# A hybrid attention layer on one Trainium2 core: where the DRAM additions, the branch operands' splits and the output slots stand in the attention steps

## The chip, the cores and the metric

The kernel runs on one core of a Trainium2 chip. The metric is the device time of one execution in microseconds: the median of three runs before the change is 1536.99 us (1536.19 to 1539.3). One further execution was taken with the hardware profiler; it took 1535.65 us.

## The reference

One layer over 1024 frames of width 1024. `h` is the RMS-normed input, and one projection gives all mixers' operands:

```
z = h @ w_in;  qa, fa, ia, ga, qb, kb, vb, gate_a, gate_b = split(z)
oa = hgrn2(qa, fa, ia, ga)                       # gated linear recurrence, 4 heads, chunks of 64
ob = band_attention(qb, kb, vb, ...)             # 8 heads of 64; each chunk sees itself and 8 chunks back
x  = x + (sigmoid(gate_a) * (oa @ w_branch_a) + sigmoid(gate_b) * (ob @ w_branch_b)) @ w_out
x  = x + (silu(h2 @ w_ffn_gate) * (h2 @ w_ffn_up)) @ w_ffn_down
x  = x + sigmoid(h3 @ w_ple_gate) * (p @ w_ple_proj)
```

In band attention q and k are RMS-normed per head, the scores get a relative-position bias, and a softmax over at most 576 keys is multiplied with v. All is in float32.

## The kernel before, in words

**Products in three parts.** Each float32 operand is kept as a rounded high part and a remainder ("hi" and "lo", type float32r), and a product is three matmuls: hi*hi, hi*lo, lo*hi. So each operand has to be split: a cast on ScalarE (ACT) for hi and a subtraction for lo on VectorE (DVE) or GpSimd (POOL).

**The order is written out by hand.** The helpers `order` (line 93), `load`, `mul`, `tr` and the pinned engines `V`, `A`, `G` chain every instruction to the one issued before it on the same engine, so PE, ACT, DVE, POOL and the DMA queue of SyncE (SP) each run in exactly the order in which the Python code emits the instructions. Semaphores between engines are made by the framework. PSUM has eight banks, handed out by `mm`; working tiles of 128x1024 come from 32 "slots", handed out by `slot`.

**The attention stage** (`attention`, line 787) is a loop over steps n = 0 to 33. Steps 0 to 31 each treat one pair of heads and one block of 128 queries: pairs 0 and 1 alternate in steps 0 to 15, pairs 2 and 3 in steps 16 to 31, and the block number grows every second step, so that steps 16 to 31 repeat the shapes of steps 0 to 15. A step emits, in this order: the loads for later steps; the rest of the softmax of step n-1; a **first unit** of the feed; the scores of step n (`scores`); in odd steps the products with v of steps n-3 and n-2 (`pv`); the transposes of q and k of step n+1 (`stack`); the splits due in this step; a **second unit** of the feed; the transposes of the probabilities of step n-1 (`pt`) and the exponentials of step n. I write 20a and 20b for the first and the second unit of step 20.

**The feed** is a stream of matmul work that fills PE between the small attention products. It gives first the q/k projection (`attn_in`, line 691; the rest of it lasts through step 19) and then `branch_a` (line 1172): `oa @ w_branch_a`, 32 units of 6 matmuls, each 128x512. After each unit, `tick` (line 199) advances all pending side jobs in `self.later` by one piece. What the loop leaves of the feed is run by `branches` (line 1199) after it. In steps 20 and 21 (`SINGLE`) the first unit is left out and only `tick` is called.

**Side jobs.** `qk_norm` (line 669) norms one finished 128x512 block k of the q/k projection: squares on ACT; one tick later a reduction on DVE and a power of -0.5 on POOL (shape 128x8); two ticks after that the row scaling on DVE, which reads the PSUM bank for the last time; two ticks later the block is stored. Blocks that finish together (k = 0, 1; 6, 7; 8, 9; 14, 15) start `late` ticks apart. `split_in` (line 895) casts a loaded head output on ACT and appends the DVE subtraction as a side job that waits for `slack`, which is set in the first half of a step. `fetch` (line 169) does the same for weights.

**Operands of branch_a.** The four head outputs `oa` were stored to DRAM; `load_in` loads them again into four slots at the end of step 13, and `SPLITS` says in which steps they are split: 18, 19, 19 and 20. The attention's own outputs `ob` take one slot for each pair of heads, at the scores of its first block (steps 0, 1, 16, 17), though the first write to it comes with `pv`, in steps 3 and 19.

**DRAM additions.** The out-projection and the down-projection need sums of quarters of their weights. `dma_sums` (line 1346) first copies quarters from DRAM to DRAM (issued by SP) and then adds others on top, with DMAs issued from POOL:

```
add = lambda out, x: self.G.dma_start(out, x, accum_op=ALU.add, max_dma_last_dim=4 * T)
```

`next(self.adds)` issues one such addition: at the start of each odd step, and in `branch_a` at the start of each of its four parts (the first of them just ahead of its first unit). Since POOL's order is fixed, a power of `qk_norm` that is emitted behind an addition can't run before that addition is issued.

Of the kernel before, what the change touches and what calls it, by code (L numbers as in the profile page):

```python
# [22 lines left out]
HALF = 512  # L23
NFF = 22
STEPS = (NFF // 2 + 1) // 2
SPLITS = (18, 19, 19, 20)
EPS = 1e-6
LEVELS = (1, 2, 4, 8, 16)
TURN = 32
# [2 lines left out]
LATE = 8  # L32
FIRST = 5
PRE = {1: (0, 1), 2: (2, 3), 9: (4, 5), 10: (6, 7)}
SINGLE = (20, 21)
GROUPS = ((0, 1), (2,), (3,), (4,), (5,), (6, 7))
RING = 4
RAW = 2
# [39 lines left out]
class Trunk:  # L78
# [612 lines left out]
    def attn_in(self):  # L691

        self.qkd = [self.spill() for _ in range(8)]
        for two in range(2):
            ws = []
            for blks in GROUPS:
                pss = []
                for j, _ in enumerate(self.tokens(ws or self.lazy(ws), blks, pss)):
                    if blks[0] == 6 and (j % 2 if two == 0 else j == 3):
                        self.fetch()  # L700
                    yield 1296
                self.later += [self.qk_norm(8 * two + b, ps, i) for i, (b, ps) in enumerate(zip(blks, pss))]

    def qk_load(self, k):
        if k < 16:
# [81 lines left out]
    def attention(self):  # L787

        steps = [(2 * two + p, b) for two in range(2) for b in range(8) for p in range(2)]
        whole = len(steps)  # L790
        feed = chain(self.feed, self.ticked(self.branch_a()))
        sc, pts = {}, {}

        def stack(n):
            if n >= whole:
                return iter(())
            p, b = steps[n]
            if b == 0:
                for h in range(2):
                    bt = self.small(640, tag="bias")  # L800
                    self.load(bt, self.d["bias"][2 * p + h])
                    self.bias[p, h] = bt
            return self.attn_stack(p, b)

        def scores(n):
            for h, stages in enumerate(self.attn_scores(*steps[n])):
                sc[n, h] = (*next(stages), stages)

        def stage(n, h):
            if 0 <= n < whole:  # L810
                next(sc[n, h][2], None)

        def pt(n, h):
            if 0 <= n < whole:
                pts[n, h] = self.attn_pt(*sc[n, h][:2])

        def pv(n):
            if 0 <= n < whole:
                self.attn_pv(*steps[n], (pts.pop((n, 0)), pts.pop((n, 1))), sc[n, 0][1])

        self.stacks = True
        self.qk_load(0)
        for i in range(4):
            next(feed, None)
            if i == 0:
                self.hgrn_gate()
            if i == 3:
                drain(stack(0))
                drain(self.hgrn_out())
        self.adds = chain(self.osum, self.wsum)  # L830
        while self.queue:
            self.rest()
        self.queue = None
        bsrc = []
        for n in range(whole + 2):
            if n % 2 and n < whole:
                next(self.adds)
            if n % 2 == 0:
                self.qk_load(n // 2 + 1)
                next(self.copies, None)  # L840
                next(self.copies, None)
            stage(n - 1, 1)
            self.slack = True
            if n in SINGLE:
                self.tick()
            else:
                next(feed, None)
            if n < whole:
                if steps[n][1] == 0:
                    self.ob.append(self.slot())  # L850
                scores(n)
            if n % 2:
                pv(n - 3)
                pv(n - 2)
            drain(stack(n + 1))
            for _ in range(SPLITS.count(n)):
                self.osrc.append(self.split_in(raws[len(self.osrc)]))
            if n in (whole - 4, whole - 3):
                bsrc.append(self.split_in(braws[len(bsrc)]))
            if n == whole:  # L860
                bsrc += [(self.slot(F32R), self.slot(F32R)) for _ in range(2)]
                self.split_half(bsrc, 0)
            self.slack = False
            next(feed, None)
            pt(n - 1, 1)
            stage(n, 0)
            stage(n, 1)
            pt(n - 1, 0)
            stage(n, 0)
            if n == 0:  # L870
                self.keep_heads(self.oa, self.od, self.done_heads)
            if n == whole // 2 + 1:
                self.keep_heads(self.ob, self.obd, [0, 1])
            if n == whole // 2 - 3:
                raws = self.load_in(self.od)
            if n == whole // 2 + 4:
                for _ in range(2):
                    self.gate_load()
            if n == whole - 6:
                braws = self.load_in(self.obd[:2])  # L880
            yield 0
        self.slack = True
        self.split_half(bsrc, 1)
        for _ in range(2):
            self.gate_load()
        self.bsrc, self.feed = bsrc, feed
# [1353 lines left out]
def drain(stream):  # L2240
    while True:
        try:
            next(stream)
        except StopIteration as e:
            return e.value
# [125 lines left out]
```

## Time and profile before

| | |
|---|---|
| median of 3 runs | 1536.99 us (1536.19 to 1539.3) |
| the profiled execution | 1535.65 us, span of its instructions 1533.7 us |
| PE / DVE / ACT / POOL busy in the span | 1510.9 / 1135.4 / 662.0 / 641.2 us |
| mean granted clock of PE | 0.998 |
| chain that ended last | PE 86%, DVE 7%, issue 3%, ACT 2%, DMA 1%, POOL 1% |

Times in the views are microseconds from the first instruction. PE is the matmul engine, PEld its weight load, SPq the queue of SyncE. In a row of the timeline stand the start, the duration, the engine, the line, the operation, out<-in by the program's tile names (`pm` a PSUM bank, `s` a slot, `m` a small tile, `wh`/`wl` and `whi`/`wlo` the two parts of weights, `d` DRAM), the shapes, a count, and in brackets the idle time before it and the instruction that ended it. In a row of the windows view stand the stretch, its length, the busy time of PE, PEld, DVE, ACT and POOL with counts, the granted clock, the DMA engines' share and GB/s. Most instructions carry line 75 or 107, which are helpers.

### The profile page before, as it was taken

What the parts mean: (1) busy time and instruction counts of PE and PEld (TensorE: products, weight loads), DVE (VectorE), ACT (ScalarE), POOL (GpSimd) and SP (SyncE); (2) the same over time, 40 slices, a digit from 0 to 9 for tenths busy, and PEclk for the clock granted to TensorE, in tenths of its full rate; (3) what the DMA queues carried; (4) which work ended last, traced back from release to release, by engine and by line L of the source; (5) the groups of instructions that cost most, each with busy time, mean ns of one, the idle gap of its engine ahead of it and who ended that gap; (6) DMA issues with size and microseconds to landing.
All of it is one profiled execution on the core that took longest, in us unless ns stands there. A gap on an engine that the chain in (4) does not pass through costs nothing.

```text
span 1533.7 us, 20820 instructions
## 1 busy us (share of the span) xinstructions
PE 1510.9 (99%) x7680; PEld 1246.9 (81%) x7680; DVE 1135.4 (74%) x1616; ACT 662.0 (43%) x1115; POOL 641.2 (42%) x365
## 2 busy tenths in 40 slices
PE   8999999999999998999999999999999999999998
PEld 6888888888887876888888888888888888888886
DVE  5778777666676767848998877777777667756678
ACT  6634333333327666733566322222222224446452
POOL 4237334500122212045223666665555545545546
PEclk9999999999999999999999999999999999999999
DMA  5557445785749779574445344443333288785325
GB/s 209 191 174 266 144 145 185 292 319 172 282 143 261 217 193 250 120 249 136 137 156 197 108 120 127 124 124 104 103 103 103 105 308 297 282 278 197 125 100 202
DMA packets 106548, 281.73 MB, mean 184 GB/s; under 512 B 11088, under 2 KB 15952, under 8 KB 105936
## 3 DMA queue, kind: packets, MB, share of 16 engines
q1 hardware_dynamic: 97600, 256.29, 47.7%
q0 software_dynamic: 8704, 24.12, 7.8%
q8 instruction: 60, 0.98, 0.3%
q14 instruction: 40, 0.33, 0.1%
q10 hardware_dynamic: 144, 0.02, 0.0%
HBM read 205.67 MB, written 106.17 MB: 203 GB/s over the span
## 4 chain that ended last, share of the span: by engine, by line
PE 86%; DVE 7%; issue 3%; ACT 2%; DMA 1%; POOL 1%; SPq 0%; DVEq 0%; ACTq 0%; POOLq 0%
PE pm L107 84%; DVE s L75 4%; PE pm L110 2%; ACT s L75 1%; DVE wl L155 0%; ACT m L75 0%; DMA wr<-in_qk 0%; DVE m L75 0%; DMA s<-in_x 0%; ACT wh L147 0%; POOL wl L155 0%; DVE q L75 0%; POOL m L75 0%; DMA wr<-in_pp 0%; DMA wr<-d 0%
## 5 line engine op out<-in xcount | busy, mean ns | idle before, releaser
L107 PE MATMUL pm<-s,whi 128*128 128x512 f32 x1904 | 586.5, 389 | 0.6 <-DVE t L75 0.6
L107 PE MATMUL pm<-s,wh 128*128 128x512 f32 (+1 forms) x1456 | 453.2, 392 | 7.4 <-ACT wh L147 5.3
L107 PEld LDWEIGHTS pm<-s,whi 128*128 128x128 f32 x1904 | 357.1, 188 | 75.4 <-DVE t L75 1.3
L107 PE MATMUL pm<-s,wlo 128*128 128x512 f32 x952 | 370.6, 389 | 0.2 <-DVE wlo L75 0.2
L75 DVE TENSOR_TENSOR s<-s,s 128x512 f32<-128x512 f32 (+3 forms) x246 | 295.6, 1232 | 64.7 <-ACT s L75 50.3
L107 PEld LDWEIGHTS pm<-s,wh 128*128 128x128 f32 x1456 | 271.8, 189 | 64.9 <-ACT wh L147 5.3
L107 PE MATMUL pm<-s,wl 128*128 128x512 f32 (+1 forms) x728 | 284.0, 390 | 0.5 <-POOL wl L155 0.5
L155 POOL TENSOR_TENSOR wl<-wr,wh 128x1024 fp32r<-128x1024 f32 (+3 forms) x71 | 176.8, 2494 | 218.6 <-ACT wh L147 213.0
L75 DVE TENSOR_TENSOR t<-pm,t 128x512 f32<-128x512 f32 x168 | 115.7, 689 | 128.6 <-PE pm L107 103.7
L107 PEld LDWEIGHTS pm<-s,wlo 128*128 128x128 f32 x952 | 178.7, 188 | 38.0 <-DVE wlo L75 0.9
L75 POOL TENSOR_TENSOR wlo<-wr,whi 128x1024 fp32r<-128x1024 f32 (+1 forms) x67 | 143.4, 2148 | 67.0 <-ACT whi L75 58.0
L107 PEld LDWEIGHTS pm<-s,wl 128*128 128x128 f32 x728 | 137.3, 189 | 29.6 <-POOL wl L155 1.2
L75 POOL TENSOR_TENSOR wlo<-q,whi 128x512 fp32r<-128x512 f32 x66 | 107.8, 1635 | 117.5 <-ACT whi L75 64.4
L147 ACT CAST wh<-wr 128x1024 fp32r<-128x1024 f32 (+2 forms) x82 | 81.1, 991 | 159.8 <-DMA wr<-d 49.2
L75 ACT CAST s<-s 128x1024 fp32r<-128x1024 f32 (+1 forms) x112 | 106.9, 976 | 64.9 <-DMA s<-d 26.6
L75 ACT CAST whi<-q 128x512 fp32r<-128x512 f32 (+1 forms) x99 | 75.0, 758 | 110.8 <-PE pm L107 87.0
L75 POOL TENSOR_TENSOR s<-t,rb 128x512 f32<-128x512 f32 x44 | 71.1, 1618 | 98.7 <-ACT t L75 98.7
L75 POOL TENSOR_TENSOR m<-m,mhalf 128x8 f32<-128x8 f32 (+1 forms) x24 | 35.9, 1520 | 158.4 <-DVE m L75 158.4
L75 ACT ACTIVATE t<-s 128x512 f32<-128x512 f32 x44 | 27.8, 632 | 159.5 <-DVE s L75 155.2
L107 PE MATMUL pm<-whi,s 128*128 128x512 f32 x256 | 91.8, 409 | 0.0
L107 PE MATMUL pm<-wh,s 128*128 128x512 f32 x256 | 88.1, 403 | 0.0
L75 DVE TENSOR_TENSOR s<-s,pm 128x512 f32<-128x512 f32 x72 | 45.5, 683 | 31.5 <-PE pm L107 31.5
(156 smaller groups left out, 1932.4 us busy)
## 6 DMA issues: line engine op xcount, KB each, us to landing
s<-d SPq DMA_DIRECT2D x81, 512.0 KB, 6.3
d<-s SPq DMA_DIRECT2D x46, 512.0 KB, 3.6
d<-s SPq DMA_DIRECT2D x87, 256.0 KB, 2.3
wr<-d SPq DMA_DIRECT2D x36, 512.0 KB, 3.5
d<-t SPq DMA_DIRECT2D x54, 256.0 KB, 4.1
wr<-in_sz SPq DMA_DIRECT2D x24, 512.0 KB, 6.7
wr<-in_sg SPq DMA_DIRECT2D x22, 512.0 KB, 3.8
wr<-in_su SPq DMA_DIRECT2D x22, 512.0 KB, 4.4
```

The source lines that it names most:

```text
L75: return lambda *a, **k: self.trunk.order(op(*a, **k), self.key)
L107: return self.order(self.nc.tensor.matmul(*a, **k))
L110: return self.order(self.nc.tensor.transpose(*a, **k))
L147: self.nc.scalar.copy(hi[:, c], raw[:, c])
L155: rest.tensor_tensor(lo[:, c], raw[:, c], f32(hi[:, c]), ALU.subtract)
```

## The change

Five edits in one place of the program:

- The addition of each odd step is issued at the end of the step and no longer at its start. The four additions of `branch_a` stay where they are in it.
- `SINGLE` goes: steps 20 and 21 have a first unit like all others, so `branch_a` begins with 20a and no longer 20b, and two units fewer are left for `branches`.
- The head outputs are loaded at the end of step 11 (before: 13) and split in steps 14, 16, 18 and 19 (before: 18, 19, 19, 20).
- A slot for `ob` is taken at the first `pv` of a pair of heads and no longer at its first scores.
- In `attn_in`, the second of two blocks that finish together (k = 1, 7, 9, 15) starts its `qk_norm` two ticks after the first and no longer one.

```
-SPLITS = (18, 19, 19, 20)
+SPLITS = (14, 16, 18, 19)
...
-SINGLE = (20, 21)
...
-                self.later += [self.qk_norm(8 * two + b, ps, i) for i, (b, ps) in enumerate(zip(blks, pss))]
+                self.later += [self.qk_norm(8 * two + b, ps, 2 * i) for i, (b, ps) in enumerate(zip(blks, pss))]
...
         def pv(n):
             if 0 <= n < whole:
+                if steps[n][1] == 0:
+                    self.ob.append(self.slot())
                 self.attn_pv(*steps[n], (pts.pop((n, 0)), pts.pop((n, 1))), sc[n, 0][1])
...
         for n in range(whole + 2):
-            if n % 2 and n < whole:
-                next(self.adds)
             if n % 2 == 0:
                 self.qk_load(n // 2 + 1)
                 next(self.copies, None)
                 next(self.copies, None)
             stage(n - 1, 1)
             self.slack = True
-            if n in SINGLE:
-                self.tick()
-            else:
-                next(feed, None)
+            next(feed, None)
             if n < whole:
-                if steps[n][1] == 0:
-                    self.ob.append(self.slot())
                 scores(n)
...
             stage(n, 0)
+            if n % 2 and n < whole:
+                next(self.adds)
...
-            if n == whole // 2 - 3:
+            if n == whole // 2 - 5:
                 raws = self.load_in(self.od)
```

Here `whole` is 32.

## The prediction

> **What bounds the kernel now.** I read the page first, then the windows view and the timelines of the attention stage.
>
> ```profile
> PE 1510.9 (99%) x7680; PEld 1246.9 (81%) x7680; DVE 1135.4 (74%) x1616; ACT 662.0 (43%) x1115; POOL 641.2 (42%) x365
> ```
>
> PE is busy for 99% of the span, so only time in which PE waits, or runs slowly, can be won. The attention loop has a built-in comparison: steps 18 to 26 have the shapes of steps 2 to 10. These windows run from the scores of step 2 to those of step 11, and from the scores of step 18 to those of step 27:
>
> ```profile
> 473.49:522.05 48.56, 47.69 (x349) 37.50 (x348) 36.80 (x125) 35.80 (x97) 10.93 (x9) 1.00 0.86 226
> 566.59:620.67 54.08, 48.57 (x338) 37.00 (x337) 39.59 (x126) 38.07 (x98) 11.87 (x11) 0.97 0.95 270
> ```
>
> The second has less matmul work (338 records against 349, because 20a and 21a are left out) and takes 5.52 us more. What a unit is worth, from the four units ahead of the loop, which lie between these two rows:
>
> ```profile
> 457.93 0.47 PE L107 MATMUL pm<-whi,s 128*128 128x512 f32 x1
> ...
> 463.50 1.26 PE L110 MATMUL pm<-eye,m 128*128 128x128 f32 x10
> ```
>
> 24 matmuls in 463.50 - 457.93 = 5.57 us make 1.39 us for a unit of six. At the first window's pace the second would take 48.56 - 2 x 1.39 = 45.78 us, so it loses 54.08 - 45.78 = **8.30 us**. Where (steps 20 and 21, two parts of step 22, then steps 4 and 5):
>
> ```profile
> 574.07:579.29 5.22, 4.04 (x19) 2.37 (x18) 4.56 (x13) 5.03 (x13) 0.21 (x1) 1.00 1.07 331
> 579.29:585.87 6.58, 6.28 (x43) 4.58 (x44) 6.12 (x21) 6.06 (x18) 0.83 (x1) 1.00 1.06 352
> 589.10:593.40 4.30, 0.55 (x3) 0.34 (x4) 2.17 (x4) 0.48 (x1) 4.30 (x4) 0.96 0.80 119
> 593.40:596.65 3.25, 3.25 (x9) 2.33 (x9) 3.10 (x12) 1.99 (x5) 0.93 (x2) 0.53 0.75 166
> 482.15:487.26 5.11, 4.51 (x25) 3.20 (x25) 4.14 (x13) 5.11 (x16) 0.00 (x0) 1.00 0.90 231
> 487.26:492.81 5.55, 5.55 (x43) 4.29 (x42) 4.78 (x14) 4.04 (x14) 4.45 (x3) 1.00 1.02 316
> ```
>
> In step 22 PE works for 0.55 of 4.30 us, and then for 3.25 us at a granted clock of 0.53. Step 20 loses 5.22 - (5.11 - 0.60 - 1.39) = 2.10 us against step 4 (0.60 is PE's idle time there, 5.11 - 4.51), and step 21 loses 6.58 - 5.55 = 1.03 against step 5, together 3.1; the rest, some 5 us, is step 22. What held it up, on POOL and then on DVE:
>
> ```profile
> 559.52 1.66 POOL L75 TENSOR_TENSOR m<-m,mhalf 128x8 f32<-128x8 f32 x1 [9.61 <-DVE m L75]
> 561.15 1.08 POOL L75 DMA_DIRECT2D d<-in_wq  x1
> 568.55 1.05 POOL L75 DMA_DIRECT2D d<-in_wq  x1 [6.32 <-issue]
> 579.08 1.04 POOL L75 DMA_DIRECT2D d<-in_wq  x1 [9.48 <-issue]
> 588.31 1.05 POOL L75 DMA_DIRECT2D d<-in_wq  x1 [8.19 <-issue]
> 588.89 3.78 POOL L75 TENSOR_TENSOR m<-m,mhalf 128x8 f32<-128x8 f32 x2
> 583.19 0.23 DVE L75 TENSOR_SCALAR m<-m,m 128x8 f32<-128x8 f32 x1
> 591.09 0.69 DVE L75 TENSOR_TENSOR m<-pm,m 128x512 f32<-128x512 f32 x1 [3.89 <-POOL m L75]
> ```
>
> The four DMA rows are the additions of steps 17, 19, 20b and 21. The first three were this long on the way:
>
> ```profile
> DMA to landing us min/median/max: 7.1/7.1/7.1
> DMA to landing us min/median/max: 10.2/10.2/10.2
> DMA to landing us min/median/max: 8.9/8.9/8.9
> ```
>
> 561.15 + 7.1, 568.55 + 10.2 and 579.08 + 8.9 each lie some 0.3 us ahead of the next issue: an addition of this kind isn't issued until the one before it has landed, and POOL stands still meanwhile. The powers of blocks 14 and 15 (x2, 588.89) stand behind the addition of step 21. Block 14's input was ready at 583.4; DVE stood 3.89 us for its power, with the softmax behind it.
>
> **The change part by part.**
>
> *Additions at the end of the step.* The same DMAs on the same queue, moved past the powers of their own step alone. By ticks, block 14 is now squared in 20a, has its power in 20b and is scaled in 21b; block 15 (two ticks behind) has its power in 21b. POOL's order becomes: addition of 19, addition of 20a, power 14, power 15, addition of 21. The addition of 20a still waits for the one of 19, until 579.08, and frees POOL at 580.1. When is power 14 due? Block 6 has the same ticks in steps 4 and 5:
>
> ```profile
> 487.01 0.23 DVE L75 TENSOR_SCALAR m<-m,m 128x8 f32<-128x8 f32 x1
> 491.78 0.68 DVE L75 TENSOR_TENSOR m<-pm,m 128x512 f32<-128x512 f32 x1
> ```
>
> Its input is ready 5.1 us and its scaling due 9.6 us behind the scores of step 4 (482.15). With 20a in front, the scores of step 20 come at 574.07 + 1.39 = 575.5, so block 14's input is ready at 580.6, its power (1.66) done at 582.2 and due at 585.1: hidden with some 2.9 us to spare, and POOL is free by 580.1 in time. Power 15 has no addition ahead of it that isn't ahead of power 14. Late next are the addition of 21 and those behind it, for which only additions wait. So the stall of step 22 goes, with its slow clock; without the cover up to all of its 5 us stays.
>
> *Splits earlier.* Each is a cast on ACT and a subtraction on DVE:
>
> ```profile
> 572.85 1.99 ACT L75 CAST s<-s 128x1024 fp32r<-128x1024 f32 x2
> 576.60 2.35 DVE L75 TENSOR_TENSOR s<-s,s 128x1024 fp32r<-128x1024 f32 x2
> ```
>
> So 1.0 and 1.2 us. The subtractions run in the first half of the next step: before in 19, 20 (two) and 21, after in 15, 17, 19 and 20. Two of them, 2.4 us of DVE, leave steps 20 and 21. Where they go there is room:
>
> ```profile
> 552.59 0.35 DVE L75 SCALAR_TENSOR_TENSOR s<-pm,cols,s 128x128 fp32r<-128x128 f32 x1 [1.40 <-ACT m L75]
> 564.36 0.35 DVE L75 SCALAR_TENSOR_TENSOR s<-pm,cols,s 128x128 fp32r<-128x128 f32 x1 [2.85 <-ACT m L75]
> 545.99 0.48 ACT L75 COPY m<-pm 128x384 f32<-128x384 f32 x1 [1.09 <-PE pm L110]
> 558.38 0.48 ACT L75 COPY m<-pm 128x384 f32<-128x384 f32 x1 [0.52 <-PE pm L110]
> ```
>
> In steps 15 and 17 DVE idles 1.40 and 2.85 us right behind the place. The casts meet 1.09 us of idle ACT in step 14 and 0.52 in step 16, where half a microsecond is pushed on. Cost: nothing; without the cover 1.2 us each.
>
> *First units in 20 and 21* bring 2.78 us of PE work forward from `branches`: nothing in sum. The one of 20a also fills the hole ahead of the scores of step 20. Of the 3.1 us of steps 20 and 21 all could stay (one subtraction remains in 20) or none. DVE's load decides; steps 4 to 7 and 20 to 23:
>
> ```profile
> 482.15:503.91 21.76, 21.16 (x157) 16.46 (x156) 16.13 (x55) 16.60 (x49) 5.55 (x4) 1.00 1.00 259
> 574.07:603.04 28.97, 23.46 (x151) 16.99 (x150) 21.40 (x67) 18.85 (x51) 7.90 (x7) 0.94 0.89 229
> ```
>
> Steps 20 to 23 will need 21.40 - 2.4 = 19.0 us of DVE, and their twins take 21.76 us. That fits at 87%, with little to spare, so I leave a third, **1.0 us** (bounds 0 and 3.1).
>
> *Slots and loads.* The four loads of `oa` move by two steps on SP,
>
> ```profile
> 528.20 1.87 SPq L102 DMA_DIRECT2D s<-d  x4
> ```
>
> 1.87 us of issue past one load of q and k and two copies, none of them due in the same step. By my count of the code, the projection's input 16, v 4, k 4, `ob` 2, loaded outputs 4 and two hi parts make just 32 slots in step 16; `ob` of pair 2, taken at its scores, would be the 33rd. Taken at `pv`, it isn't. Cost: nothing; at worst half a step, some 2.5 us, if my count is one short.
>
> *Blocks 1, 7, 9 and 15 a tick later.* Each holds its PSUM bank half a step longer. Blocks 0 and 1 pass in the recurrence, ahead of the loop:
>
> ```profile
> 431.65 0.67 DVE L75 TENSOR_REDUCE m<-m 128x8 f32<-128x512 f32 x1
> 433.35 1.29 DVE L75 TENSOR_TENSOR s<-s,s 128x512 f32<-128x512 f32 x2
> 434.80 1.16 PE L107 MATMUL pm<-s,m 128*128 128x128 f32 x8 [1.30 <-ACT m L75]
> ```
>
> Their two reductions take 433.35 - 431.65 = 1.70 us of DVE, and PE waits 1.30 us behind them. One now goes behind the next level: up to 0.85 us won, or up to a unit, 1.39 us, lost if the bank is missed. I take half of the 0.85, **0.4 won**. For blocks 7 and 9 the first window holds 48.56 - 47.69 = 0.87 us of PE idle in all; I leave it (bounds: all won, or as much again lost).
>
> **The sum.** 8.30 - 1.0 + 0.4 = 7.7 us. Behind the loop PE has no gaps to speak of,
>
> ```profile
> 660.31:1533.70 873.39, 865.32 (x3852) 715.69 (x3850) 652.36 (x674) 339.86 (x455) 447.47 (x236) 1.00 0.49 166
> ```
>
> so the gain should reach the end. The profiled execution took 1535.65 us (1533.7 of span, 1.95 around it) and would take 1527.9; the median of the runs lies 1.34 above it: 1536.99 - 7.7 = **1529.3 us**. With all bounds at once the gain is between 8.30 - 3.1 - 2.5 - 1.39 - 0.87 = 0.4 and 8.30 + 0.85 + 0.87 = 10.0; not all of them hold together, and leaving the slot's 2.5 aside, my own range for this case is 2.9 to 10.0.
>
> A rule of the Trainium skill speaks against this. The page "SBUF — State Buffer", section "SBUF: two separate sides", says that a VectorE operation with two SBUF inputs and a GpSimd operation that reads SBUF exclude each other for a whole instruction. By it the two powers would meet DVE's subtractions, up to 1.66 us, and the sum would be 1531.0. In the rows the two powers at 588.89 took 1.89 us each beside a standing DVE and the one at 559.52 took 1.66 beside a working one; none shows a block, and I give it no share.
>
> **The rivals.**
>
> *The queue stays the bound* (0.12). Power 14 still stands behind two additions, now back to back. Landings differ by 3.1 us (7.1 to 10.2), my spare is 2.9, and a half clock would follow. A stall of half the old size leaves about half the gain: 1533.
>
> *Without effect, or given back* (0.10). Two units less behind the loop are 2.78 us less cover for the weights of the next product, and stages that follow DMAs might not move up: up to 7.7 back, 1537. Against it: the row of PE behind the loop, 8 us idle in 873.
>
> *PSUM banks become the bound, and it is slower* (0.11). Banks held longer, and two half-done products from 20a on, leave fewer than PE wants: in step 21, blocks 14 and 15, two halves, two scores, two products with v and one transpose are nine of eight. PE then waits until DVE has read the scores, four reads like
>
> ```profile
> 510.86 0.55 DVE L75 CUSTOM_DVE_ANT_0 m<-pm,m 128x384 f32<-128x384 f32 x1
> ```
>
> or 2.2 us each time, in steps 6, 10, 20, 21 and 22, and 1.39 in the recurrence: 12.4 against 7.7, so 1541.7. From the fourth such wait on it is slower. Against it: steps 4 and 5 hold as many banks, with 0.60 us idle.
>
> **How the numbers follow.** My forecast has 0.67, with 1527.0 to 1534.1 as its own range. Eight times in ten takes in the queue's case and part of the second: 1525.8 to 1537.0. A measurement of this kernel tells about 0.2% (3.1 us) from no change. Faster: nearly all of the forecast and most of the queue's case, 0.77; same: the second case and what is left of those, 0.13; slower: 0.10, most of the third.
>
> **What would show it.** In the changed profile the powers of blocks 14 and 15 run ahead of the addition of step 21 and apart; DVE has no wait for POOL in the loop; steps 18 to 26, with two units more, take 48 to 50 us at a clock of 1.00; DVE's subtractions in 15 and 17 delay no matmul. I am wrong if PE waits microseconds for a PSUM reader in steps 6, 10 or 20 to 22, if power 14 still ends later than its scaling is due, or if the loop gains and the end doesn't.

## The result and the profile after

| | before | after |
|---|---|---|
| median of 6 runs beside each other | 1537.35 us | 1528.6 us |
| lowest to highest | 1536.19 to 1539.3 | 1526.33 to 1529.18 |
| ratio, 95% interval | | 0.9939 (0.9926 to 0.9952) |
| the profiled execution | 1535.65 us | 1528.95 us |

By the medians 8.75 us are won; the forecast was 7.7 and 1529.3 us. The two profiled executions are 6.7 us apart, and their spans 1533.7 - 1526.9 = 6.8. All readings of "after" below are of the execution of 1528.95 us. The helpers stand one line higher in the changed program: L74 is L75 of before, L106 is L107, L109 is L110.

The page: busy time, and the chain that ended last.

```profile
span 1526.9 us, 20819 instructions
PE 1509.6 (99%) x7680; PEld 1247.0 (82%) x7680; DVE 1130.0 (74%) x1616; ACT 662.6 (43%) x1115; POOL 643.3 (42%) x365
PE 94%; DVE 3%; DMA 1%; ACT 1%; issue 0%; SPq 0%; POOL 0%; DVEq 0%; POOLq 0%; ACTq 0%
```

PE's busy time hardly changes (1510.9 before). In the chain the 3% of "issue" (46 us) is gone; about half of it was POOL standing ahead of its additions (6.30 + 9.47 + 8.18 = 23.95 us in the chain of before). DVE falls from 7% to 3%.

The windows view of after, cut at the same scores as in the prediction: steps 2 to 10, steps 18 to 26, then steps 19, 20, 21 and 22 alone. The columns are stretch, length, busy time of PE, PEld, DVE, ACT and POOL, granted clock, DMA share and GB/s.

```profile
473.78:522.35 48.57, 47.48 (x350) 37.54 (x350) 36.67 (x124) 35.82 (x97) 10.63 (x9) 1.00 0.85 217
566.91:615.39 48.48, 47.56 (x350) 37.53 (x350) 37.99 (x124) 36.04 (x96) 10.94 (x10) 1.00 0.98 284
570.82:576.75 5.93, 5.01 (x33) 3.56 (x32) 4.44 (x13) 4.81 (x17) 0.00 (x0) 1.00 1.07 328
576.75:581.07 4.32, 4.32 (x25) 3.21 (x24) 3.92 (x12) 3.15 (x11) 1.28 (x2) 1.00 1.04 370
581.07:586.62 5.55, 5.55 (x43) 4.29 (x42) 4.52 (x12) 4.73 (x15) 1.45 (x1) 1.00 1.07 338
586.62:591.34 4.72, 4.72 (x34) 3.73 (x33) 4.36 (x17) 3.23 (x9) 3.36 (x3) 1.00 0.33 89
```

The two halves now have the same matmuls (350 records) and the same length, 48.57 and 48.48 us, at a clock of 1.00. The second took 54.08 with two units less; with those taken off again it is 48.48 - 2.78 = 45.70, so 54.08 - 45.70 = **8.38 us** are won there. In steps 20 to 22 PE is busy all the time. The 0.92 us without PE are in step 19.

The timelines of after: POOL, then DVE, then PE, with the idle time before a row and what ended it in brackets.

```profile
568.86 1.05 POOL L74 DMA_DIRECT2D d<-in_wq  x1 [6.33 <-issue]
579.79 1.04 POOL L74 DMA_DIRECT2D d<-in_wq  x1 [9.87 <-issue]
580.81 1.71 POOL L74 TENSOR_TENSOR m<-m,mhalf 128x8 f32<-128x8 f32 x1
587.04 1.64 POOL L74 TENSOR_TENSOR m<-m,mhalf 128x8 f32<-128x8 f32 x1 [4.52 <-DVE m L74]
589.62 1.10 POOL L74 DMA_DIRECT2D d<-in_wq  x1 [0.94 <-issue]
```

```profile
580.43 0.23 DVE L74 TENSOR_SCALAR m<-m,m 128x8 f32<-128x8 f32 x1
...
585.36 0.68 DVE L74 TENSOR_TENSOR m<-pm,m 128x512 f32<-128x512 f32 x1
...
587.39 1.22 DVE L74 TENSOR_TENSOR wl<-wr,wh 128x1024 fp32r<-128x1024 f32 x1
```

```profile
434.38 1.13 PE L106 MATMUL pm<-s,m 128*128 128x128 f32 x8 [0.43 <-ACT m L74]
...
443.31 1.16 PE L106 MATMUL pm<-s,m 128*128 128x128 f32 x8 [0.50 <-DVE s L74]
...
573.16 0.44 PE L109 MATMUL pm<-eye,m 128*128 128x128 f32 x2 [0.92 <-DMA m<-d]
```

The addition of 20a still waits 9.87 us for the one ahead of it. Power 14 follows it at once and is done at 580.81 + 1.71 = 582.5; its scaling starts at 585.36 without a wait (before: after 3.89 us of standing). Power 15 stands alone, ahead of the addition of 21. PE's 1.30 us in the recurrence became 0.43, but 0.50 us appear at a later product of it. The one gap left in the second half waits for a DMA, a load of q or k.

Not all of the 8.38 us is seen at the end of this execution. Step 2 starts 0.3 us later than before (473.78 against 473.49); 0.44 us of delay are there at 14.73 us already (14.29 before), where the program is the same. And 8.38 - 0.3 - 6.8 = 1.3 us are lost behind these steps: some 0.5 of them ahead of a product that starts at 812.46 (819.99 before), the other 0.7 behind it, where this execution has one stretch of slow clock that the one of before has not (its rows are in the last section).

### The profile page after: what moved, and what is told of

Its sections match the earlier page's. It is cut to its first block, busy times and chain, and to the rows that moved or that the text cites. A ratio compares the mean times of both kernels' runs of the same rounds, so it can differ in the third digit from the quotient of the medians.

```text
span 1526.9 us, 20819 instructions
## 1 busy us (share of the span) xinstructions
PE 1509.6 (99%) x7680; PEld 1247.0 (82%) x7680; DVE 1130.0 (74%) x1616; ACT 662.6 (43%) x1115; POOL 643.3 (42%) x365
## 4 chain that ended last, share of the span: by engine, by line
PE 94%; DVE 3%; DMA 1%; ACT 1%; issue 0%; SPq 0%; POOL 0%; DVEq 0%; POOLq 0%; ACTq 0%
PE pm L106 91%; PE pm L109 3%; DVE s L74 2%; DMA m<-d 1%; DMA wr<-in_qk 0%; DMA s<-in_x 0%; DVE m L74 0%; ACT s L74 0%; ACT m L74 0%; DVE s L393 0%; DVE wl L74 0%; DVE s L290 0%; SPq L101 0%; DVE pm L74 0%; ACT wh L146 0%
## 5 line engine op out<-in xcount | busy, mean ns | idle before, releaser
L106 PE MATMUL pm<-s,whi 128*128 128x512 f32 x1904 | 586.2, 389 | 0.0
L106 PE MATMUL pm<-s,wh 128*128 128x512 f32 (+1 forms) x1456 | 452.9, 392 | 6.5 <-ACT wh L146 5.3
L106 PEld LDWEIGHTS pm<-s,whi 128*128 128x128 f32 x1904 | 357.3, 188 | 74.4 <-DVE t L74 0.4
L106 PE MATMUL pm<-s,wlo 128*128 128x512 f32 x952 | 370.6, 389 | 0.0
L74 DVE TENSOR_TENSOR s<-s,s 128x512 f32<-128x512 f32 (+3 forms) x246 | 291.8, 1216 | 63.9 <-ACT s L74 49.6
L106 PEld LDWEIGHTS pm<-s,wh 128*128 128x128 f32 x1456 | 271.3, 189 | 63.6 <-ACT wh L146 5.3
L106 PE MATMUL pm<-s,wl 128*128 128x512 f32 (+1 forms) x728 | 283.8, 390 | 0.5 <-POOL wl L154 0.5
L74 DVE TENSOR_TENSOR t<-pm,t 128x512 f32<-128x512 f32 x168 | 115.7, 688 | 130.2 <-PE pm L106 105.6
L106 PEld LDWEIGHTS pm<-s,wlo 128*128 128x128 f32 x952 | 178.7, 188 | 37.7 <-DVE wlo L74 0.5
L74 POOL TENSOR_TENSOR wlo<-wr,whi 128x1024 fp32r<-128x1024 f32 (+1 forms) x67 | 143.5, 2150 | 67.0 <-ACT whi L74 58.0
L106 PEld LDWEIGHTS pm<-s,wl 128*128 128x128 f32 x728 | 137.2, 188 | 29.4 <-POOL wl L154 1.2
L74 POOL TENSOR_TENSOR wlo<-q,whi 128x512 fp32r<-128x512 f32 x66 | 107.8, 1635 | 117.5 <-ACT whi L74 64.4
L74 ACT CAST s<-s 128x1024 fp32r<-128x1024 f32 (+1 forms) x112 | 107.1, 977 | 67.3 <-DMA s<-d 26.7
L74 ACT CAST whi<-q 128x512 fp32r<-128x512 f32 (+1 forms) x99 | 75.0, 758 | 111.1 <-PE pm L106 87.1
L74 POOL TENSOR_TENSOR s<-t,rb 128x512 f32<-128x512 f32 x44 | 71.2, 1620 | 99.3 <-ACT t L74 99.3
L74 POOL TENSOR_TENSOR m<-m,mhalf 128x8 f32<-128x8 f32 (+1 forms) x24 | 35.9, 1498 | 163.5 <-DVE m L74 163.5
L74 ACT ACTIVATE t<-s 128x512 f32<-128x512 f32 x44 | 27.8, 633 | 158.6 <-DVE s L74 154.5
L106 PE MATMUL pm<-whi,s 128*128 128x512 f32 x256 | 91.8, 409 | 0.0
L106 PE MATMUL pm<-wh,s 128*128 128x512 f32 x256 | 88.1, 403 | 0.0
L74 DVE TENSOR_TENSOR s<-s,pm 128x512 f32<-128x512 f32 x72 | 45.9, 681 | 34.3 <-PE pm L106 34.3
```

The lines of the kernel that those rows point to most:

```text
L74: return lambda *a, **k: self.trunk.order(op(*a, **k), self.key)
L106: return self.order(self.nc.tensor.matmul(*a, **k))
```

## The experiments

The times are medians with their ratio to the kernel before, run beside them.

| kernel | us | ratio (95%) |
|---|---|---|
| additions at the end alone | 1532.24 | 0.9970 (0.9958 to 0.9981) |
| after, additions back at the start | 1529.19 | 0.9951 (0.9937 to 0.9964) |
| early loads, splits and late slots alone | 1538.16 | 1.0006 (0.9997 to 1.0014) |
| after, two additions ahead of power 14 | 1535.7 | 0.9990 (0.9981 to 0.9999) |
| after, one tick | 1528.02 | 0.9944 (0.9931 to 0.9956) |
| after, `SINGLE` back | 1530.28 | 0.9954 (0.9941 to 0.9968) |
| after, slots at the scores | 1529.46 | 0.9945 (0.9933 to 0.9958) |
| after, a store one step later | 1527.88 | 0.9939 (0.9926 to 0.9951) |
| before, room for more additions | 1539.45 | 1.0016 (1.0007 to 1.0024) |
| after, room for more additions | 1537.0 | 0.9998 (0.9989 to 1.0007) |

My theory: power 14 behind a waiting addition is most of the loss; the early splits and the first units are the rest; ticks and slots hardly count. The rivals give the gain to the lightened DVE, to the ticks or to the banks.

**The additions alone.** The kernel before, with one edit:

```
-            if n % 2 and n < whole:
-                next(self.adds)
 ...
+            if n % 2 and n < whole:
+                next(self.adds)
```

> The kernel before with the additions moved to the end of odd steps, and nothing else. POOL's order becomes: addition of 20b, power 14, power 15, addition of 21. Theory of the queue (a power is late only when an addition that still waits for its forerunner stands ahead of it): power 14, ready at 583.4, runs at once, DVE has no wait for POOL, the stall of step 22 and its slow clock go (some 5 us), and the 3.1 us of steps 20 and 21 stay: about 1532, ratio 0.9967. Rival that steps 20 and 21 alone made step 22 late (DVE overloaded by the splits): little changes, 1536 to 1538. Rival that the place of the additions carries all: 1529.

1532.24 us, 5.1 less than before. POOL's timeline in this kernel:

```profile
581.53 1.22 POOL L75 DMA_DIRECT2D d<-in_wq  x1 [10.40 <-issue]
584.79 1.67 POOL L75 TENSOR_TENSOR m<-m,mhalf 128x8 f32<-128x8 f32 x1 [2.04 <-DVE m L75]
587.11 1.64 POOL L75 TENSOR_TENSOR m<-m,mhalf 128x8 f32<-128x8 f32 x1 [0.65 <-DVE m L75]
589.14 1.10 POOL L75 DMA_DIRECT2D d<-in_wq  x1 [0.39 <-issue]
```

The powers now wait only for their own input, from DVE. What is left in steps 20 and 21 is PE waiting, for DVE above all:

```profile
579.10 0.50 PE L107 MATMUL pm<-s,wh 128*128 128x512 f32 x1 [0.74 <-DVE s L75]
...
581.45 0.70 PE L107 MATMUL pm<-s,m 64*128 64x384 f32 x4 [0.31 <-DVE s L75]
```

So the queue was worth the 5 us of step 22, and steps 20 and 21 are a matter of their own. PE's waits in steps 20 and 21 are those of the kernel before (0.74 and 0.30 us there).

**Everything but the additions.** The changed kernel, with the first edit undone:

```
+            if n % 2 and n < whole:
+                next(self.adds)
 ...
-            if n % 2 and n < whole:
-                next(self.adds)
```

> The changed kernel with the additions back at the start of odd steps, all else as changed. Power 14 then stands ahead of the addition of 21 anyway (20b is ahead of 21), and only power 15 goes behind it. Theory of the queue: the addition of 21 is issued at about 589.6, power 15 runs at 590.2 to 591.9 and its scaling was due at 591.6, so at most half a microsecond is lost: 1528.5 to 1529.5, no difference from the changed kernel that can be measured. Rival that moving the additions to the end is what won the 5 us: 1533 to 1534.

1529.19 us, level with 1528.6. The move of the additions, enough alone, isn't needed beside the other edits:

```profile
579.80 1.04 POOL L74 DMA_DIRECT2D d<-in_wq  x1 [9.97 <-issue]
580.38 2.15 POOL L74 TENSOR_TENSOR m<-m,mhalf 128x8 f32<-128x8 f32 x1
588.18 1.10 POOL L74 DMA_DIRECT2D d<-in_wq  x1 [5.65 <-DVE m L74]
588.83 2.15 POOL L74 TENSOR_TENSOR m<-m,mhalf 128x8 f32<-128x8 f32 x1
```

With a first unit in step 20 the last pieces of the projection are handed over half a step sooner, in 20a instead of 20b. Power 14 comes in 20b and is so ahead of the addition of step 21 in either place. A kernel with the first units as its only edit was not run.

**The early splits without the queue's mending.** The kernel before, with these edits (`ob` slots at `pv` too):

```
-SPLITS = (18, 19, 19, 20)
+SPLITS = (14, 16, 18, 19)
 ...
-            if n == whole // 2 - 3:
+            if n == whole // 2 - 5:
                 raws = self.load_in(self.od)
```

> The kernel before with the early loads and splits and the slots at the first product with v; additions, single units and ticks as before. Theory of the queue: PE loses less in steps 20 and 21, but power 14 still waits for the chain of additions, which isn't earlier (589 to 591), so what is won ahead of it is waited for there: 1536 to 1537.5, ratio 0.999 to 1.000. Rival that the parts add up: 2 to 3 us won, 1534.5.

1538.16 us: nothing won. POOL, DVE and PE:

```profile
589.99 1.05 POOL L75 DMA_DIRECT2D d<-in_wq  x1 [7.34 <-issue]
590.58 3.77 POOL L75 TENSOR_TENSOR m<-m,mhalf 128x8 f32<-128x8 f32 x2
...
592.77 0.69 DVE L75 TENSOR_TENSOR m<-pm,m 128x512 f32<-128x512 f32 x1 [5.79 <-POOL m L75]
...
567.71 0.62 PE L107 MATMUL pm<-s,m 64*128 64x256 f32 x6
...
593.51 0.55 PE L110 MATMUL pm<-eye,s 128*128 128x128 f32 x3 [4.65 <-DVE m L75]
```

DVE's wait for the power grew by 1.9 us, from 3.89 to 5.79. Counted from the scores of step 18 (567.71 here, 566.59 before), DVE comes to this wait 1.3 us sooner (19.3 us against 20.6), and the addition of 21 goes out 0.6 us later (22.3 against 21.7), since the ones before it landed later. So what was won ahead of the queue was waited for at the queue: the addition of 21 goes out when the one before has landed, not when PE is there. The parts don't add up: alone the splits give nothing, behind a mended queue they do (below).

**Two additions ahead of power 14.** The changed kernel, the addition of step 21 moved to 20a, beside the one that is there:

```
-            if n % 2 and n < whole:
+            if n % 2 and n < whole and n != 21:
                 next(self.adds)
 ...
+            if dd == 0:
+                next(self.adds)
```

> The changed kernel with one addition moved: that of step 21 is issued in 20a, behind the one that stands there, so two of them wait ahead of power 14. Nothing else differs. Theory of the queue: the second can't be issued before the first has landed (589.6 in the trace of the changed kernel), power 14 ends at about 592 where it was due at 585.4, DVE stands some 6 us and PE some 5 to 7 with a slow clock behind it: 1534 to 1536. Rival (additions don't hold up the powers; the splits or the left-out units did it): no change, 1528.6.

1535.7 us: one DMA's place in POOL's order costs 7.1 us against 1528.6. POOL, DVE and PE:

```profile
579.98 1.04 POOL L74 DMA_DIRECT2D d<-in_wq  x1 [9.90 <-issue]
589.00 1.05 POOL L74 DMA_DIRECT2D d<-in_wq  x1 [7.99 <-issue]
589.59 2.16 POOL L74 TENSOR_TENSOR m<-m,mhalf 128x8 f32<-128x8 f32 x1
...
591.78 0.69 DVE L74 TENSOR_TENSOR m<-pm,m 128x512 f32<-128x512 f32 x1 [7.56 <-POOL m L74]
...
592.53 0.69 PE L109 MATMUL pm<-eye,m 128*128 128x128 f32 x2 [6.14 <-DVE m L74]
```

This is the chain of before, rebuilt within the changed kernel: addition, power, scaling, PE.

**One tick.** The changed kernel, with

```
-... self.qk_norm(8 * two + b, ps, 2 * i) ...
+... self.qk_norm(8 * two + b, ps, i) ...
```

> The changed kernel with the second of two blocks one tick behind the first again (i for 2 * i). The power of block 15 is then emitted in 21a, still ahead of the addition of 21. Theory: no difference in the loop; in the recurrence PE's wait of 0.43 us near 434 grows back to 1.3 and the one of 0.50 near 443 goes, so some 0.1 to 0.4 us slower, which the times can't tell: 1528.3 to 1529.5. Rival that the second tick keeps two reductions from piling up in step 21: 1 to 2 us slower.

1528.02 us, level with 1528.6. PE's wait in the recurrence is back:

```profile
434.75 1.16 PE L106 MATMUL pm<-s,m 128*128 128x128 f32 x8 [1.29 <-ACT m L74]
```

and the 0.50 us at 443.31 are gone. The second tick moves a wait and takes 1.29 - 0.43 - 0.50 = 0.36 us off it. The stretch around it gets only 0.12 us shorter: from the start of the first wait to the product near 453 it is 452.91 - 433.46 = 19.45 us with one tick and 453.28 - 433.95 = 19.33 with two. That is too little to be told in the times.

**`SINGLE` back.** The changed kernel, with

```
+SINGLE = (20, 21)
 ...
-            next(feed, None)
+            if n in SINGLE:
+                self.tick()
+            else:
+                next(feed, None)
```

> The changed kernel with the first units of steps 20 and 21 left out again, all else as changed. POOL: power 14 ahead of the addition of 21, power 15 behind it but due late. Theory: the units' work is only moved (nothing in sum), but the hole ahead of the scores of step 20, which 20a filled, is back, 1 to 2 us: 1529.6 to 1530.8. Rival that the early splits alone win the 3.1 us of steps 20 and 21: 1528.6, no difference.

1530.28 us. The scores of step 20, PE's waits in step 22 and the scores of step 23:

```profile
574.41 1.26 PE L107 MATMUL pm<-s,m 64*128 64x384 f32 x6
...
585.71 0.44 PE L110 MATMUL pm<-eye,m 128*128 128x128 f32 x2 [0.27 <-DVE s L75]
...
588.43 0.55 PE L110 MATMUL pm<-eye,m 128*128 128x128 f32 x3 [0.57 <-ACT m L75]
...
590.31 1.21 PE L107 MATMUL pm<-s,m 64*128 64x256 f32 x12
```

From the scores of step 20 to those of step 23 it takes 590.31 - 574.41 = 15.90 us. The changed kernel takes 591.34 - 576.75 = 14.59 with one unit more, which is worth 1.39 us. So 2.7 us are lost, and the two waits in step 22 are only 0.84 of them; the rest stands inside longer rows, such as the scores of step 20 (1.26 us here, 0.80 in the changed kernel).

So the gain has three steps: the additions alone 1537.3 to 1532.24; with early splits (and slots and ticks) 1530.28; with the first units 1528.6. The last two steps, 2.0 and 1.7 us, have ratios whose intervals overlap, and the traces share them out otherwise. Steps 18 to 26, with 2.78 us added where two units are missing, take 48.97 + 2.78 = 51.75 us with the additions alone, 48.19 + 2.78 = 50.97 with `SINGLE` back and 48.48 in the changed kernel: 0.8 and 2.5 us. The sum of the two, 3.3 to 3.6 us, is sound; their shares are open.

**Slots at the scores.** The changed kernel, with

```
-                if steps[n][1] == 0:
-                    self.ob.append(self.slot())
                 self.attn_pv(...)
 ...
+                if steps[n][1] == 0:
+                    self.ob.append(self.slot())
                 scores(n)
```

> The changed kernel with the slots of ob taken at the first scores again. By the count of slots in the prediction the hi part of the split in step 16 is then the 33rd of 32 and ACT's cast waits for a slot of the projection's input, which the matmuls of 16b release, at once or 1 to 2.5 us late: 1528.5 to 1531, with a wait of that cast for PE in the trace. Rival that the count is wrong and slots are free: no wait there and 1528.6.

1529.46 us, no difference. The cast of step 16, which would have to wait for a 33rd slot, starts at 558.33, and at 558.03 in the changed kernel's trace. By the prediction, missing a slot for half a step would have cost some 2.5 us.

**A store one step later.** The outputs `ob` of pairs 0 and 1 are stored by SP at the end of step 17, just ahead of the load for which PE waits 0.92 us. The changed kernel, with

```
-            if n == whole // 2 + 1:
+            if n == whole // 2 + 2:
```

> The changed kernel with the store of the first two ob (keep_heads) one step later, at the end of step 18, so that SP's load of q and k for step 20 no longer stands behind it. Theory: PE's wait of 0.92 us for a DMA at the transposes of step 20 goes: 1527.7, shown by the trace, too little for the times to tell. Rival that the load is late through the traffic of other DMAs and not through SP's order: the wait stays.

1527.88 us against 1528.6 of the changed kernel, each with a spread of over 1 us: not told apart. In the trace the wait is gone, and SP's order shows what the store does: in the changed kernel this load is issued at 564.37, behind the two stores at 562.85, and with the stores later it is issued at 558.78. But the wait is also gone with one tick and with the additions at the start, where the store stays. Behind the store, the load takes about 6 to 7 us to land in the profiles without the wait, and 8.3 to 9.0 us in the three with it (the changed kernel, 8.7; with the slots at the scores; with `SINGLE` back). So the store takes the slack, and the time on the way decides; what makes that differ from profile to profile is open.

**Room for more additions.** So far an addition was issued only when the one before had landed. Is that a rule of such DMAs, or is there room for one only? The kernel sets how much memory POOL's DMAs have for their descriptors. In the kernel before, and in the changed one:

```
-    nc = bacc.Bacc("TRN2", ..., dynamic_dma_scratch_size=1024)
+    nc = bacc.Bacc("TRN2", ..., dynamic_dma_scratch_size=2048)
```

> The kernel before with twice the memory for the descriptors of POOL's DMAs (2048 bytes for 1024), nothing else changed. My theory by now: an addition isn't issued before the one ahead of it has landed because there is room for one only. With room for two, the addition of step 21 goes out without the 8.19 us of standing, powers 14 and 15 end some 5 us sooner, DVE's wait of 3.89 us for POOL is gone, and the kernel takes what additions at the end of odd steps alone gave, 1532 (1530.5 to 1533.5). Rival: an addition waits for the landing of the one ahead whatever the room; then POOL still stands 6 to 10 us ahead of the additions and the time is that of before, 1537.3 within 1.

> The changed kernel with twice the memory for the descriptors of POOL's DMAs. By my theory POOL no longer stands ahead of its additions, but nothing of this kernel waits for POOL there any more: 1528.6, within 1. By the rival theory, that the standing still costs something elsewhere in this kernel (weights' copies on POOL later, or the d<-d additions in a later stage), it is faster than 1527.

1539.45 and 1537.0 us: both expectations of the time fell. The kernel before is 2.4 us slower with more room, and the changed kernel loses its whole gain, 8.4 us. In the kernel before with more room, the timelines of POOL, PE and the SP queue:

```profile
563.22 3.25 POOL L75 DMA_DIRECT2D d<-in_wq  x3
571.09 1.03 POOL L75 DMA_DIRECT2D d<-in_wq  x1 [4.62 <-issue]
592.07 1.67 POOL L75 TENSOR_TENSOR m<-m,mhalf 128x8 f32<-128x8 f32 x1 [19.94 <-DVE m L75]
...
579.57 0.69 PE L110 MATMUL pm<-eye,m 128*128 128x128 f32 x2 [5.56 <-DMA m<-d]
...
566.14 0.81 SPq L102 DMA_DIRECT2D m<-d  x1
```

In the changed kernel with more room, POOL and PE, and then its windows view around PE's wait:

```profile
562.75 3.24 POOL L74 DMA_DIRECT2D d<-in_wq  x3
...
579.44 0.69 PE L109 MATMUL pm<-eye,m 128*128 128x128 f32 x2 [5.90 <-DMA m<-d]
```

```profile
572.00:582.00 10.00, 4.10 (x22) 2.95 (x22) 4.25 (x11) 3.41 (x11) 0.00 (x0) 0.71 1.07 316
```

The same load on the SP queue of the changed kernel with the room that it had:

```profile
564.37 0.80 SPq L101 DMA_DIRECT2D m<-d  x1
```

One half of the mechanism is as I had it: with room, additions go out back to back and no power waits for one. The size of the room is not: I had expected two, and three fit. The fourth goes out at 571.09, just after the first, 7.6 us on the way, has landed (563.22 + 7.6 = 570.8).

What I had missed is that POOL had been holding them apart. These additions wait for nothing else, so POOL, free from step 17 on, issues those of steps 17, 19 and 20b (20a in the changed kernel) within 3.3 us. The load of q or k for which PE waits is issued at 566.14, behind them, and takes 13.4 us to land (13.7 in the changed kernel with more room, 8.7 with less). PE waits 5.56 or 5.90 us for it, where the changed kernel waited 0.92, and then runs on at a slow clock (a mean of 0.71 over 572 to 582).

So the bunched additions make this load late, since nothing else was edited. That they do so by taking the DMA engines from it is likely but not shown: the engines' share is 1.07 here, and 1.07 in step 19 of after as well. Nor is the load the whole loss: with more room, in the changed kernel PE waits 1.23 and 1.38 us in step 4, where it had waited 1.09 in all.

## Why the prediction was right, and where it was not

**The stall of step 22** was read rightly, in its cause and in its size. The additions alone give 5.1 us where "some 5 us" stood, and putting one addition back ahead of power 14 costs 7.1. The due times held to a few tenths: input ready at 580.43 + 0.23 = 580.7 (580.6 predicted), power done at 582.5 (582.2), scaling at 585.36 (585.1). There is luck in this. The scores of step 20 came at 576.75, not at 575.5, because of the late load and the later start, and the input was ready 3.9 us behind them, not 5.1; the two errors cancel.

**Which edit does it** was put down too narrowly. The prediction said that by ticks the power comes in 20b, and gave the gain to the additions' move. The first unit in step 20 makes the same order, since it hands the projection's last blocks over half a step sooner; with it and the other edits, the additions may stay at the start (1529.19).

**The pace of the first half as the measure** held: 48.48 us against 48.57. Of the 8.30 us to be won, all were won (8.38). The **1.0 us left in steps 20 and 21** was not there: PE has no idle time in either. Before, PE's waits there were for DVE above all (e.g. 0.74 and 0.31 us with the additions alone), so "DVE's load decides" was right for the kernel before. The early splits and the first units together ended these waits; taking a third of 3.1 as lost was too careful. In the changed kernel DVE still works 3.92 of 4.32 us in step 20 and 4.52 of 5.55 in step 21, without holding PE up. What did stay, 0.92 us in step 19, has another cause that the prediction didn't have, a late load.

**The sum** came out near the measured time partly by luck. Its 1.0 us of loss was none, its 0.4 us from the second tick was about 0.1, and "the gain should reach the end" put at nothing the 1.3 us that this execution lost behind the steps. The gain of 7.7 us lies between the 6.8 of the two spans and the 8.75 of the medians.

**The splits hidden in steps 14 to 17** cost nothing, as said. From 522 to 566 in the windows view of after, PE is busy throughout:

```profile
522.00:566.00 44.00, 44.00 (x391) 36.64 (x390) 32.64 (x110) 29.55 (x76) 10.25 (x8) 1.00 0.70 200
```

**The slots.** The count of 32 with `ob` as "the 33rd" did not show: taken at the scores, it delays nothing. Either a slot is free then or one is freed in time; which of the two is open. Its edit is worth nothing measurable.

**The second tick.** Half of 0.85 us was taken, 0.4. It takes 0.36 us of waits out of the recurrence, which gets 0.12 us shorter, and the times show nothing. For blocks 7 and 9, a wait of 0.27 us at 511.47 in the profile before is gone; with one tick in the changed kernel it is back (0.28 at 511.84). PE's wait in step 4 is 5.60 - 4.51 = 1.09 us, against 0.60 before, as the row of that step has it:

```profile
482.43:488.03 5.60, 4.51 (x25) 3.20 (x24) 4.23 (x14) 5.60 (x18) 0.00 (x0) 1.00 0.93 248
```

That is not the tick's work: the wait is 1.05 us with one tick in the changed kernel, and lies between 0.59 and 1.27 in all kernels here with the smaller room. The **banks' rival** isn't seen: in the steps that it named, PE waits microseconds for no PSUM reader. The **queue's rival** is what the two additions ahead of power 14 make: it needs one more DMA in front than the change has. **Given back** didn't happen: steps 18 to 26 end earlier and so does the kernel, but for the 1.3 us that this one execution lost behind them.

**The Trainium skill's rule** ("SBUF — State Buffer", section "SBUF: two separate sides") would have cost up to 1.66 us. Here power 15 runs from 587.04 for 1.64 us, and DVE's subtraction with two SBUF inputs lies within it, from 587.39 for 1.22, each as long as without the other (1.66 and 1.2 in the prediction's rows). No exclusion for a whole instruction is seen with these two. That is so for a power of 128x8; with larger operations it may not be: in the same trace a DVE operation with two SBUF inputs (`s<-t,s`, 128x512) takes 0.69 us at 923.08, without one of POOL beside it, and 1.42 at 918.37, beside POOL's subtractions. One reading in the prediction was off: of its two powers at 588.89, only the first ran beside a standing DVE, which works again from 591.09.

**What would have been wrong next.** The prediction took POOL's standing for pure loss, to be moved past. The runs with more room show that it also spread the additions over time. The change was right to leave the standing where it was and only to take the powers out from behind it.

## What to carry to other kernels

On an engine that runs in a fixed order, an instruction that depends on nothing is issued as soon as the engine is free, whatever step it was written in; find what stands behind it, and put the short work with a due time ahead. Before removing the wait of a DMA queue, ask what that wait keeps apart: here the stall came back at a load. Where a loop repeats the same shapes, its undisturbed half tells what the disturbed half can win, to a few tenths of a microsecond here; and parts that sit on one chain (the splits, behind the queue) were worth nothing here until the later wait was gone.

## What was not expected of the hardware

- **The spacing of POOL's additions follows the room for descriptors.** With 1024 bytes they go out one by one, 7 to 11 us apart in the loop's second half (561.45, 568.86, 579.79 and 589.62 in the changed kernel); with 2048, three go out within 3.3 us (`x3` at 563.22), and only the fourth waits 4.62 us. The Trainium skill ("DMA: Bandwidth & Descriptors", section "SWDGE vs HWDGE vs iDMA") says that GpSimd writes the descriptors of its DMAs into rings of a reserved part of SBUF; that the issue follows the size of this part agrees with it.
- **A slow clock behind a gap of a quarter of a microsecond.** The windows view, first of after, then of before:

```profile
810.00:820.00 10.00, 9.74 (x47) 8.17 (x46) 9.14 (x11) 8.35 (x14) 3.87 (x2) 0.83 0.42 111
```

```profile
810.00:820.00 10.00, 9.74 (x53) 8.29 (x51) 7.88 (x11) 7.14 (x12) 0.00 (x0) 1.00 0.15 55
820.00:830.00 10.00, 10.00 (x52) 8.55 (x53) 9.90 (x10) 7.28 (x12) 3.85 (x2) 1.00 0.66 205
```

The same 0.26 us without PE stand in both, ending at 812.46 in after and at 819.99 in before, so that in before the next row is the one behind the gap. In after the granted clock is 0.50 from about 813 to 816.5, a mean of 0.83 over the row, which costs at most 0.17 x 9.74 = 1.7 us of work; some of that is won back at a wait of 0.57 us at 844.46, which before has and after has not. The kernel with `SINGLE` back has the slow stretch too, and so has the one with early splits alone; the profiles of the other kernels here have the gap at a clock of 1.00. Just ahead of the gap stand sixteen products with one output column each, 1.84 us in all, in after as in before, so these alone don't decide it. What decides isn't settled.

The stretch is not the main reason why the gain by two profiles (6.7 us) is smaller than by the medians (8.75). Of these 2.05 us, 1537.35 - 1535.65 = 1.70 are that the profiled execution of before was faster than its median, and 0.35 that the one of after was slower than its own.
